# A decoder layer on one core: the cumulative product's idle operand, and the norm of a stick-breaking unit

## The chip, the cores and the metric

The kernel runs on one core of one Trainium2 chip. The core has TensorE (PE: matmuls; PEld is its weight load), VectorE (DVE), ScalarE (ACT), GpSimd (POOL) and SyncE (SP), whose queue issues the DMAs. The metric is the time of one execution in microseconds on the device. Before the change it is 3093.26 us, the median of three runs (3088.63 to 3095.98).

## What is computed

One decoder layer over 2048 positions of width 1024, in f32. A norm and one projection give queries, keys and values. Four heads do differential attention, with a softmax. Eight heads of width 64 do stick-breaking attention. The outputs are joined, projected, normed and added; a gated MLP with a short convolution follows, and has the larger half of the matmuls. The part that matters here is this, cut from the reference:

```python
z = jnp.einsum('bhqd,bhkd->bhqk', q_blk, k).astype(jnp.float32) * scale
log_beta = jax.nn.log_sigmoid(z)
log_1mb = jnp.where(strict, jax.nn.log_sigmoid(-z), 0.0)
between = lax.cumsum(log_1mb, axis=3, reverse=True) - log_1mb
a = jnp.where(strict, jnp.exp(log_beta + between), 0.0)
return jnp.einsum('bhqk,bhkd->bhqd', a.astype(v.dtype), v)
...
sb_o = _rmsnorm(_stick_breaking_attention(sq, sk, sv), sb_norm[l])
```

Each query row needs, for every key, the product of sigmoid(-z) over the later keys: the kernel works with sigmoids and a running product in place of logarithms and sums. Each head's 64 outputs are then normed and multiplied by the 64 gains sb_norm.

## The kernel before

**Stages.** Projection passes go first (L605, L602). From then on, attention and the remaining projections are merged step by step, so that projection matmuls fill TensorE's gaps: differential attention for four pairs of heads, then stick-breaking for four pairs. The output projection (L1101) is merged into the end of stick-breaking, and the MLP (L1226, L1311) comes last. A unit is a pair of heads g with 256 query rows s; stick-breaking has 32 units.

**Order of work.** The code doesn't issue instructions as it runs. Each step is an operation with an engine (or two to choose from), a cost, its dependencies and its buffers, and a planner (class `Plan`) lays them out when the kernel is built: an engine takes the oldest ready operation whose buffers fit. So the order on each engine's queue is fixed at build, and at run time each engine follows its queue and waits on semaphores. Buffers are counted: z has three PSUM banks, t (transposes) two, o and g a few more. A PSUM buffer is marked `bank`, and the planner does not start an operation on it while another engine's is under way. `copy` may go to ACT or DVE.

**Stick-breaking, per chunk.** A chunk is up to 512 keys of one head for 128 rows; there are 320 (224 with 512 keys, 32 each with 384, 256 and 128). In `front`: L702 computes z into PSUM, two matmuls, since the query is split in a high and a low part (L705 adds the mask on the diagonal); L969 writes sigmoid(-z) to the tile gm in SBUF and L971 sigmoid(z) to the tile be, both on ACT; L977 is the running product over gm, backward, on DVE, in place, starting from the chunk before (`carry`); L982 multiplies be by it on POOL. gm and be are parts of two rings of SBUF, `a` and `w`. Two units later the rows are transposed (L720), evacuated as high part (L466 or L467) and low part (L734), and multiplied with the values into o (L1000).

The product, with its operand gm read twice and the second one not used (`bypass`):

```python
gr = gm.t[:, 0:w + 1][:, ::-1]
nc.vector.tensor_tensor_scan(gr, gr, gr, 1.0 if cb is None else cb[0].t[:, 0:1],
                             ALU.mult, ALU.bypass)
```

**Stick-breaking, the end of a unit.** `fin_sb` (L793) evacuates o, transposes it in four pieces (L799), and gets for each query row and each of four pieces 64 values twice, from the high and the low part of the value product. A copy takes the second half and L804 (DVE) adds the first; L806 squares (POOL), L807 sums (DVE), L382 scales and adds epsilon (DVE), L384 takes the power -1/2 (POOL), and L816, four times, multiplies a piece by its row's factor and by the gains, which lie in `sbn` across all partitions. `mix_out` (L758) transposes the result (L763), copies it to SBUF and stores it. `mix_out` is also used by differential attention (`fin_diff`, L768).

Of the kernel before, what the change touches and what calls it, by code (L numbers as in the profile page):

```python
# [24 lines left out]
P = 128  # L25
# [241 lines left out]
def layer_kernel(  # L267
# [167 lines left out]
    def setup_rest():  # L435
# [11 lines left out]
        mem["sbn"] = load(lambda: sbn, sb_norm[0:1, :].to_broadcast([P, 64]), 32768)  # L447
# [310 lines left out]
    def mix_out(g, s, mx, deps):  # L758
# [6 lines left out]
        o = copy(lambda: mo.t, lambda: ps.t[:, 0:256], 256, (o,), (ps, mo))  # L765
# [27 lines left out]
    def fin_sb(g, s, po, last):  # L793
        ot, pq, os_, ss, sq, mx = buf("ot"), buf("t"), buf("os"), small(), buf("sq"), buf("mix")
# [6 lines left out]
        p4 = lambda: pq.t.rearrange("p (c l d) -> p c l d", c=4, l=2)  # L801
        o4 = lambda: os_.t.rearrange("p (c d) -> p c d", c=4)
# [3 lines left out]
        o = op("POOL", c_pool(256), lambda: nc.gpsimd.tensor_tensor(sq.t, os_.t, os_.t, ALU.mult), (o,), (os_, sq))  # L806
        o = op("DVE", 335, lambda: nc.vector.reduce_sum(ss.t[:, 0:4], sq.t.rearrange("p (c d) -> p c d", c=4),  # L807
                                                        axis=AX.X), (o,), (sq, ss))
        r, o = rs_ops(lambda: ss.t[:, 0:4], 64, 4, (o,), (ss,))

        def fin():
            m4 = mx.t.rearrange("p (j m d) -> p j m d", j=2, m=2)
            for m in range(2):
                for jj in range(2):
                    c = m * 2 + jj
# [612 lines left out]
```

## Time and profile before

| what | value |
|---|---|
| median of 3 runs | 3093.26 us |
| the profiled execution | 3094.23 us |
| its span in the profile | 3092.5 us |
| PE busy | 2984.5 us (97%) |
| DVE busy | 2252.0 us (73%) |
| ACT busy | 1442.9 us (47%) |
| POOL busy | 951.6 us (31%) |
| mean granted TensorE clock | 0.992 of full |

The profile is of one execution. An engine is busy while an instruction's record lasts, so a record that contains a wait inside the engine counts as busy, and matmul records overlap, their ends being modelled. The shares are averages over stages with different limits; the tables by stretch of time are what to read; there, behind the engines, stand the granted clock as a share, the share of the DMA engines and GB/s. In a row of a group, "xcount | busy, mean ns | idle before" is followed by what ended the idle time.

### The profile page before, as it was taken

The page shows a single profiled execution, that of the slowest core. Times are in us where ns is not written, and L with a number is a line of the kernel's source. Part 1 is how long each engine was busy: PE and PEld are TensorE (multiplying, and loading weights), DVE is VectorE, ACT ScalarE, POOL GpSimd, SP SyncE. Part 2 cuts the span into 40 slices and gives each one's busy share as a digit, 9 for nine tenths or more (in the row PEclk, how much of TensorE's full clock was granted, in tenths as well). Part 3 has the DMA queues.
Part 4 walks back from the last instruction along what each step waited for, and adds up shares of the span by engine and source line. Part 5 has one row for each costly group of instructions (what it writes and reads, how often), then busy time and mean ns, then how long its engine had stood idle before and what let it go on. Part 6 is the DMA issues. An engine that isn't in the chain of part 4 may idle for free. (4 is left out here: it accounts for less than half of the span.)

```text
span 3092.5 us, 48117 instructions
## 1 busy us (share of the span) xinstructions
PE 2984.5 (97%) x17352; PEld 2610.4 (84%) x17352; DVE 2252.0 (73%) x4327; ACT 1442.9 (47%) x2913; POOL 951.6 (31%) x1047
## 2 busy tenths in 40 slices
PE   7999999999999999889999999999999999999998
PEld 7899999999888888868877888888888888888887
DVE  4658878897999999998754864387744776277742
ACT  4434545555777767666643433233322433233321
POOL 1001002002766777675411211033301332023310
PEclk9999999999999999999999999999999999999999
DMA  8776656655634366533363333443344333343332
GB/s 264 246 209 186 185 151 201 171 156 159 188 122 130 95 194 185 151 100 112 110 214 126 102 100 116 121 134 96 96 129 143 96 99 106 119 141 101 96 123 82
DMA packets 392146, 437.11 MB, mean 141 GB/s; under 512 B 20096, under 2 KB 328164, under 8 KB 381668
## 3 DMA queue, kind: packets, MB, share of 16 engines
q1 hardware_dynamic: 391908, 434.05, 46.7%
q8 instruction: 136, 2.23, 0.3%
q14 instruction: 102, 0.84, 0.1%
HBM read 333.30 MB, written 100.67 MB: 140 GB/s over the span
## 5 line engine op out<-in xcount | busy, mean ns | idle before, releaser
L1226 PE MATMUL pu<-fh,fhi 128*128 128x512 f32 x2816 | 869.0, 390 | 0.2 <-ACT fu L1234 0.2
L1226 PEld LDWEIGHTS pu<-fh,fhi 128*128 128x128 f32 x2816 | 529.4, 188 | 110.5 <-ACT fu L1234 0.6
L461 DVE TENSOR_TENSOR flo<-fraw,fhi 128x1024 fp32r<-128x1024 f32 x186 | 233.0, 1254 | 488.6 <-ACT fhi L458 488.5
L1226 PE MATMUL pu<-fh,flo 128*128 128x512 f32 x1408 | 549.2, 390 | 0.0
L982 POOL TENSOR_TENSOR ring_w<-ring_w,ring_a 128x512 f32<-128x512 f32 (+2 forms) x320 | 387.9, 1224 | 220.3 <-DVE ring_a L977 121.1
L605 PE MATMUL g<-hT,big 128*128 128x256 f32 x3072 | 447.8, 288 | 7.3 <-DVE st L638 4.3
L458 ACT CAST fhi<-fraw 128x1024 fp32r<-128x1024 f32 x253 | 265.5, 1051 | 397.4 <-PE py L1311 218.6
L1311 PE MATMUL py<-fhi,gt 128*128 128x512 f32 x1408 | 435.9, 390 | 0.0
L605 PEld LDWEIGHTS g<-hT,big 128*128 128x128 f32 x3072 | 405.4, 192 | 19.8 <-DVE st L638 4.4
L977 DVE TENSOR_TENSOR_SCAN ring_a<-ring_a 128x513 f32<-128x513 f32 (+2 forms) x320 | 412.8, 1316 | 6.1 <-ACT ring_a L969 6.1
L702 PE MATMUL z<-k,q 128*128 128x512 f32 (+3 forms) x1280 | 362.5, 376 | 10.4 <-ACT ring_a L969 7.0
L466 ACT CAST thi<-t 128x512 fp32r<-128x512 f32 (+2 forms) x472 | 221.6, 492 | 210.1 <-PE t L720 179.3
L1311 PEld LDWEIGHTS py<-fhi,gt 128*128 128x128 f32 x1408 | 264.5, 188 | 60.0
L1226 PEld LDWEIGHTS pu<-fh,flo 128*128 128x128 f32 x1408 | 264.7, 188 | 54.9
L734 DVE TENSOR_TENSOR tlo<-t,thi 128x512 fp32r<-128x512 f32 (+2 forms) x528 | 281.6, 556 | 34.6 <-ACT thi L466 28.4
L459 POOL TENSOR_TENSOR flo<-fraw,fhi 128x1024 fp32r<-128x1024 f32 x78 | 195.8, 2510 | 338.9 <-DVE fhi L457 171.2
L1311 PE MATMUL py<-flo,gt 128*128 128x512 f32 x704 | 277.8, 395 | 0.0
L720 PE MATMUL t<-ident,ring_w 128*128 128x128 f32 x1632 | 253.2, 276 | 22.4 <-DVE tlo L734 18.5
L1250 POOL TENSOR_TENSOR gt<-fy,gt 128x512 fp32r<-128x512 f32 x88 | 118.4, 1347 | 493.9 <-ACT gt L1249 483.0
L1239 DVE SCALAR_TENSOR_TENSOR fy<-fu,cw,fy 128x512 f32<-128x512 f32 x176 | 239.6, 1361 | 6.2
L384 POOL TENSOR_TENSOR sm<-sm,neghalf 128x2 f32<-128x2 f32 (+1 forms) x72 | 76.8, 1067 | 536.5 <-DVE sm L382 534.7
L602 PE MATMUL g<-big,hT 128*128 128x256 f32 x1536 | 227.4, 288 | 6.3 <-DVE st L624 1.5
(158 smaller groups left out, 4697.4 us busy)
## 6 DMA issues: line engine op xcount, KB each, us to landing
fraw<-in_w_up_dram SPq DMA_DIRECT2D x176, 512.0 KB, 3.8
hT<-hd SPq DMA_DIRECT2D x64, 1024.0 KB, 7.0
fraw<-in_w_down_dram SPq DMA_DIRECT2D x88, 512.0 KB, 3.8
q<-qd SPq DMA_DIRECT2D x128, 256.0 KB, 4.3
hd<-hT SPq DMA_DIRECT2D x16, 1024.0 KB, 5.4
qd<-st SPq DMA_DIRECT2D x128, 128.0 KB, 2.6
kd<-st SPq DMA_DIRECT2D x128, 128.0 KB, 2.6
vd<-st SPq DMA_DIRECT2D x64, 256.0 KB, 5.2
```

Of the source, the lines that this page charges most:

```text
L458: "ACT", c_act(n) + 42, lambda: nc.scalar.copy(hi(), raw()))
L461: "DVE", c_dvs(n), lambda: nc.vector.tensor_tensor(lo(), raw(), f32(hi()), ALU.subtract))
L602: nc.tensor.matmul(ps.t[:, cs], hk[:, b, c * P:(c + 1) * P], wv[:, a, k, :], start=first, stop=last)
L605: nc.tensor.matmul(ps.t[:, cs], wv[:, a, k, c * P:(c + 1) * P], hk[:, b, :], start=first, stop=last)
L702: nc.tensor.matmul(ps.t[:, 0:w], q.t[:, m, l, jj * P:(jj + 1) * P], kt.t[:, m, 0:w], start=(l == 0), stop=(l == 1 and not masked))
L720: nc.tensor.transpose(ps.t[:, cc * P:(cc + 1) * P], rows[jj].t[:, (k + kk) * P:(k + kk + 1) * P], ident)
L734: ol = op("DVE", c_dvp(n), lambda sl=sl: nc.vector.tensor_tensor(lo.t[:, sl], ps.t[:, sl], f32(hi.t[:, sl]), ALU.subtract), (oh,), (ps, hi ...
L977: nc.vector.tensor_tensor_scan(gr, gr, gr, 1.0 if cb is None else cb[0].t[:, 0:1], ALU.mult, ALU.bypass)
L982: rdeps.append(op("POOL", c_pool(w), lambda be=be, gm=gm, w=w: nc.gpsimd.tensor_tensor(be.t, be.t, gm.t[:, 1:w + 1], ALU.mult), (o1, o2), ...
L1226: nc.tensor.matmul(ps.t, w3(w)[:, k, :], h.t[:, a, k, :], start=(k == 0 and i == 0), stop=(k == KD - 1 and i == 2))
L1239: nc.vector.scalar_tensor_tensor(y.t, u.t[:, 1:TT + 1], cw[:, 1, f:f + 1], y.t, ALU.mult, ALU.add)
L1311: nc.tensor.matmul(ps.t, gt.t[:, a, j * P:(j + 1) * P], wt.t[:, ms], start=(m == 0 and i == 0), stop=(m == NFT - 1 and i == 2))
```

## The change

The product's second operand becomes the first column of the z tile in PSUM, repeated; the product thus reads that tile and is one of its users. In a unit's end, the four transposes become four multiplications with `fold`, an identity of 64 stacked on itself, which adds the two halves; a plain copy evacuates the sum. The scale of the mean and the epsilon move to one POOL operation, with 64 and the factor 8 taken into `sbn`, which now holds the gains down the partitions, twice. One DVE operation multiplies all four pieces by their row factors. The gains are applied in `mix_out` by the evacuation after the transpose, where they lie down the partitions: on ACT, or on DVE.

```diff
-    sbn = const.tile([P, 64], F32, name="sbn")
+    sbn = const.tile([P, 1], F32, name="sbn")
+    fold = const.tile([P, 64], F32, name="fold")
+    nc.vector.tensor_tensor(fold, ident[:, 0:64], ident[:, 64:P], ALU.add)
...
-        mem["sbn"] = load(lambda: sbn, sb_norm[0:1, :].to_broadcast([P, 64]), 32768)
+        ls = [load(lambda m=m: sbn[m * 64:(m + 1) * 64], sb_norm.rearrange("o p -> p o"), 256) for m in range(2)]
+        mem["sbn"] = op("DVE", 75, lambda: nc.vector.tensor_scalar(sbn, sbn, 8.0, None, ALU.mult), ls)
...
+        if scale is None:
+            o = copy(lambda: mo.t, lambda: ps.t[:, 0:256], 256, (o,), (ps, mo))
+        else:
+            o = op("ACT", c_act(256) + 95, lambda: nc.scalar.activation(
+                mo.t, ps.t[:, 0:256], AF.Identity, scale=sbn[:, 0:1]), (o, scale), (ps, mo)).alt(
+                "DVE", c_dvp(256), lambda: nc.vector.tensor_scalar(mo.t, ps.t[:, 0:256], sbn[:, 0:1], None, ALU.mult))
...
-                nc.tensor.transpose(pq.t[:, c * P:(c + 1) * P], ot.t[:, c * P:(c + 1) * P], ident)
+                nc.tensor.matmul(pq.t[:, c * 64:(c + 1) * 64], ot.t[:, c * P:(c + 1) * P], fold, start=True, stop=True)
...
-        o = copy(o4, lambda: p4()[:, :, 1, :], 256, (o,), (pq, os_))
-        o = op("DVE", c_dvp(256), lambda: nc.vector.tensor_tensor(o4(), p4()[:, :, 0, :], o4(), ALU.add), (o,),
-               (pq, os_))
+        o = copy(lambda: os_.t, lambda: pq.t[:, 0:256], 256, (o,), (pq, os_))
...
-        r, o = rs_ops(lambda: ss.t[:, 0:4], 64, 4, (o,), (ss,))
+        def pw():
+            nc.gpsimd.tensor_scalar(t.t[:, 0:4], ss.t[:, 0:4], 64 * EPS, None, ALU.add)
+            nc.gpsimd.tensor_tensor(r.t[:, 0:4], t.t[:, 0:4], neghalf[:, 0:4], ALU.pow)
+        o1 = op("POOL", 1200, pw, (o1,), (ss, t, r))
...
-                    nc.vector.scalar_tensor_tensor(m4[:, jj, m, :], o4()[:, c, :], r.t[:, c:c + 1], sbn,
-                                                   ALU.mult, ALU.mult)
-        o = op("DVE", 4 * 196, fin, (o, mem["sbn"]), (r, os_, mx))
+            nc.vector.tensor_tensor(
+                mx.t.rearrange("p (j m d) -> p j m d", j=2, m=2),
+                os_.t.rearrange("p (m j d) -> p j m d", m=2, j=2),
+                r4.unsqueeze(3).to_broadcast([P, 2, 2, 64]), ALU.mult)
+        o = op("DVE", 396, fin, (o1,), (r, os_, mx))
+        mix_out(g, s, mx, (o,), mem["sbn"])
...
-                    nc.vector.tensor_tensor_scan(gr, gr, gr, 1.0 if cb is None else cb[0].t[:, 0:1],
-                                                 ALU.mult, ALU.bypass)
-                o1 = op("DVE", c_scan(w), scan, [o0, o1] + ([cb[1]] if cb else []), [gm] + ([cb[0]] if cb else []),
-                        what="scan")
+                    nc.vector.tensor_tensor_scan(gr, gr, ps.t[:, 0:1].to_broadcast([P, w + 1]),
+                                                 1.0 if cb is None else cb[0].t[:, 0:1], ALU.mult, ALU.bypass)
+                o1 = op("DVE", c_scan(w), scan, [o0, o1] + ([cb[1]] if cb else []),
+                        [gm, ps] + ([cb[0]] if cb else []), what="scan")
```

## Rows read from the trace of the kernel before

**Rows 1.** Stretches: us; busy us (instructions) of PE, PEld, DVE, ACT, POOL; then the clock.

```profile
250.00:450.00 200.00, 199.84 (x1547) 192.44 (x1546) 169.16 (x574) 97.30 (x215) 11.25 (x11) 1.00 0.62 170
738.00:800.00 62.00, 61.57 (x500) 59.80 (x500) 48.21 (x84) 36.56 (x96) 29.57 (x46) 1.00 0.66 189
800.00:1350.00 550.00, 503.07 (x3721) 460.64 (x3720) 537.61 (x779) 401.37 (x914) 397.12 (x561) 0.99 0.51 151
1350.00:1531.00 181.00, 168.01 (x945) 141.46 (x944) 154.98 (x219) 112.46 (x275) 104.58 (x137) 0.97 0.30 98
...
1700.00:3092.50 1392.50, 1383.44 (x6082) 1142.44 (x6080) 856.79 (x1223) 463.75 (x655) 320.99 (x181) 1.00 0.37 111
```

**Rows 2.** DVE's groups by line, stretch 738 to 1531 (first two: L977).

```profile
L977 DVE TENSOR_TENSOR_SCAN ring_a<-ring_a 128x513 f32<-128x513 f32 (+2 forms) x320 | 412.8, 1316 | 6.1 <-ACT ring_a L969 6.1
...
L977 DVE TENSOR_TENSOR_SCAN ring_a<-ring_a 128x513 f32<-128x513 f32 x224 | 327.7, 1481 | 4.5 <-ACT ring_a L969 4.5
...
L816 DVE SCALAR_TENSOR_TENSOR mix<-os,sm,sbn 128x64 f32<-128x64 f32 x124 | 54.4, 497 | 3.2 <-POOL ring_a L967 2.3 <-POOL sm L384 0.8
...
L804 DVE TENSOR_TENSOR os<-t,os 128x256 f32<-128x256 f32 x31 | 12.5, 403 | 1.5 <-ACT os L466 1.3
L382 DVE TENSOR_SCALAR sm<-sm 128x4 f32<-128x4 f32 (+1 forms) x32 | 12.2, 380 | 0.5 <-ACT sq L780 0.4
```

**Rows 3.** Timeline of DVE and POOL: start us, us, instruction.

```profile
1006.85 1.28 DVE L977 TENSOR_TENSOR_SCAN ring_a<-ring_a 128x513 f32<-128x513 f32 x1
1008.04 1.69 DVE L816 SCALAR_TENSOR_TENSOR mix<-os,sm,sbn 128x64 f32<-128x64 f32 x4
...
1016.40 1.47 DVE L977 TENSOR_TENSOR_SCAN ring_a<-ring_a 128x513 f32<-128x513 f32 x1
...
1018.38 1.46 DVE L977 TENSOR_TENSOR_SCAN ring_a<-ring_a 128x513 f32<-128x513 f32 x1
...
1002.30 1.09 POOL L982 TENSOR_TENSOR ring_w<-ring_w,ring_a 128x512 f32<-128x512 f32 x1 [1.11 <-PE z L702]
...
1016.79 1.98 POOL L982 TENSOR_TENSOR ring_w<-ring_w,ring_a 128x512 f32<-128x512 f32 x1
```

**Rows 4.** TensorE's transposes of attention rows, 800 to 1350, then 250 to 450.

```profile
L720 PE MATMUL t<-ident,ring_w 128*128 128x128 f32 x849 | 132.5, 276 | 14.6 <-DVE tlo L734 12.7 <-DVE sm L382 0.5 <-DVE os L804 0.4
...
L720 PE MATMUL t<-ident,ring_w 128*128 128x128 f32 x178 | 27.1, 273 | 0.0
```

**Rows 5.** First sigmoids (L969, two rows), products (L977, two rows) since 738, counted.

```profile
738.00:950.00 212.00, 50.42 (x96) 1.00 0.56 165
...
738.00:1200.00 462.00, 110.52 (x210) 1.00 0.52 154
...
738.00:950.00 212.00, 113.94 (x90) 1.00 0.56 165
...
738.00:1200.00 462.00, 258.83 (x203) 1.00 0.52 154
```

**Rows 6.** Waits, whole span: who for whom, us in total, times, longest.

```profile
POOL ring_w L982 <- DVE ring_a L977: 121.1, 88, 3.5
...
ACT r L1117 <- DVE r L1115: 13.3, 8, 3.8
```

**Rows 7.** Groups by line and shape, whole span (L422: its source view).

```profile
L971 ACT ACTIVATE ring_w<-z 128x512 f32<-128x512 f32 x224 | 134.0, 613 | 9.0 <-PE z L702 7.7 <-PE z L705 0.6
...
L574 ACT ACTIVATE hT<-t,g_pre 128x256 fp32r<-128x256 f32 x64 | 25.9, 473 | 29.3 <-PE t L567 19.3 <-PE g L602 9.9
...
L734 DVE TENSOR_TENSOR tlo<-t,thi 128x512 fp32r<-128x512 f32 x336 | 223.2, 676 | 29.9 <-ACT thi L466 26.0 <-PE o L911 1.5 <-PE o L1000 1.2
...
L1248 DVE TENSOR_TENSOR fy<-fy,fy 128x512 f32<-128x512 f32 x88 | 65.2, 742 | 2.8 <-DVE fu L1232 0.4
...
L384 POOL TENSOR_TENSOR ws<-ws,neghalf 128x1 f32<-128x1 f32 x32 | 21.0, 656 | 66.6 <-DVE ws L382 61.9 <-DVE fu L1232 4.8
...
L422 PE MATMUL t<-ring_w,sm x2: 481/482/482, 87.0 to 87.3; 32*4 32x384 f32 x2
```

More of the change, by code (lines that the diff above doesn't have):

```diff
@@ L756, in layer_kernel, with mix_out @@
     mixs = {}
-    def mix_out(g, s, mx, deps):
+    def mix_out(g, s, mx, deps, scale=None):
         ps, mo = buf("t"), buf("mo")
@@ L793, in fin_sb @@
     def fin_sb(g, s, po, last):
-        ot, pq, os_, ss, sq, mx = buf("ot"), buf("t"), buf("os"), small(), buf("sq"), buf("mix")
+        ot, pq, os_, ss, sq, mx, r = buf("ot"), buf("t"), buf("os"), small(), buf("sq"), buf("mix"), small()
         o = copy(lambda: ot.t, lambda: po.t, 512, (last,), (po, ot))
@@ L804, in fin_sb @@
-        o = op("DVE", c_dvp(256), lambda: nc.vector.tensor_tensor(o4(), p4()[:, :, 0, :], o4(), ALU.add), (o,),
-               (pq, os_))
-        o = op("POOL", c_pool(256), lambda: nc.gpsimd.tensor_tensor(sq.t, os_.t, os_.t, ALU.mult), (o,), (os_, sq))
-        o = op("DVE", 335, lambda: nc.vector.reduce_sum(ss.t[:, 0:4], sq.t.rearrange("p (c d) -> p c d", c=4),
-                                                        axis=AX.X), (o,), (sq, ss))
-        r, o = rs_ops(lambda: ss.t[:, 0:4], 64, 4, (o,), (ss,))
@@ L811, in fin @@
-        def fin():
[L812 to L815, printed above, removed]
-                    nc.vector.scalar_tensor_tensor(m4[:, jj, m, :], o4()[:, c, :], r.t[:, c:c + 1], sbn,
-                                                   ALU.mult, ALU.mult)
-        o = op("DVE", 4 * 196, fin, (o, mem["sbn"]), (r, os_, mx))
-        mix_out(g, s, mx, (o,))
+        o = copy(lambda: os_.t, lambda: pq.t[:, 0:256], 256, (o,), (pq, os_))
@@ new lines, in fin_sb @@
+        o1 = op("POOL", c_pool(256), lambda: nc.gpsimd.tensor_tensor(sq.t, os_.t, os_.t, ALU.mult), (o,), (os_, sq))
+        o1 = op("DVE", 335, lambda: nc.vector.reduce_sum(ss.t[:, 0:4], sq.t.rearrange("p (c d) -> p c d", c=4),
+                                                         axis=AX.X), (o1,), (sq, ss))
+        t = small()
+        def pw():
+            nc.gpsimd.tensor_scalar(t.t[:, 0:4], ss.t[:, 0:4], 64 * EPS, None, ALU.add)
+            nc.gpsimd.tensor_tensor(r.t[:, 0:4], t.t[:, 0:4], neghalf[:, 0:4], ALU.pow)
@@ L821, in layer_kernel @@
+        o1 = op("POOL", 1200, pw, (o1,), (ss, t, r))
+        def fin():
+            r4 = r.t[:, 0:4].rearrange("p (m j) -> p j m", m=2)
+            nc.vector.tensor_tensor(
[4 more added lines that the diff above has]
+        mix_out(g, s, mx, (o,), mem["sbn"])
     LEAD = {"z": 0.0, "ev": 0.0}
@@ L973, in front, with scan @@
                 cb = None if diag else carry[m, jj]
-                def scan(gm=gm, w=w, cb=cb):
+                def scan(gm=gm, w=w, cb=cb, ps=ps):
                     gr = gm.t[:, 0:w + 1][:, ::-1]
-                    nc.vector.tensor_tensor_scan(gr, gr, gr, 1.0 if cb is None else cb[0].t[:, 0:1],
-                                                 ALU.mult, ALU.bypass)
-                o1 = op("DVE", c_scan(w), scan, [o0, o1] + ([cb[1]] if cb else []), [gm] + ([cb[0]] if cb else []),
-                        what="scan")
+                    nc.vector.tensor_tensor_scan(gr, gr, ps.t[:, 0:1].to_broadcast([P, w + 1]),
+                                                 1.0 if cb is None else cb[0].t[:, 0:1], ALU.mult, ALU.bypass)
+                o1 = op("DVE", c_scan(w), scan, [o0, o1] + ([cb[1]] if cb else []),
+                        [gm, ps] + ([cb[0]] if cb else []), what="scan")
                 carry[m, jj] = (gm, o1)
```

3 lines of the change are left out of this document (removed).

## The prediction

> **What bounds the kernel now.** I read the table of stages first. From 1700 us to the end, in the MLP, TensorE is busy 1383.44 of 1392.50 us, so nothing there can be gained by VectorE work [rows 1]. Stick-breaking runs from 738 to 1531 us. TensorE is busy 61.57 of 62 us in the first stretch, but 503.07 of 550 and 168.01 of 181 us in the next two: 0.4 + 46.9 + 13.0 = 60.3 us idle. VectorE is busy 537.61 of the 550 us (98%); ScalarE has 401 and POOL 397. The stretch 250 to 450, in differential attention, is what to hold beside it: VectorE at 85% (169.16 of 200) and TensorE never idle [rows 1]. So between 800 and 1350 VectorE sets the pace.
>
> Next, what VectorE does there. The cumulative products (L977) are 412.8 us, and the norm of a unit (L804, L382, L816) 12.5 + 12.2 + 54.4 us [rows 2]. A product over 513 elements costs 327.7/224 = 1.46 us on average, though alone it takes 1.19 us to the next start (1006.85 to 1008.04). The timeline shows why: while POOL multiplies, each product reads 1.46 or 1.47 us and the POOL instruction 1.98 us in place of 1.09 [rows 3]. The two engines' records overlap, and the lengths add up as if they took turns. Both instructions read two SBUF operands. The evacuation of the same size with one PSUM operand (L734) has a mean of 0.676 us, below the 0.742 us of a two-SBUF one (L1248) [rows 7].
>
> **The change, part by part.**
>
> *The product's unused operand.* The multiplication and the bypass stay, but the second stream comes from a PSUM column. If turn-taking with POOL goes, 224 products save 1.46 - 1.19 = 0.27 us: 61 us. The 96 shorter ones take (412.8 - 327.7)/96 = 0.89 us; they have 257 elements on average, half of 513, so an estimate from 1.19 us is about 0.64 with a fixed part, and they save 0.25 each: 24 us. Together 85 us of VectorE. The price of the PSUM read is not in the trace. From below: nothing, and no further gain beyond the 0.066 us that separates L734 from L1248, 320 times, 21 us. From above: the read costs as much as a whole L734 beside the product, 1.19 + 0.68 = 1.87 us, then 224 products lose 0.41 each and the short ones (0.64 + 0.34 against 0.89) 0.09 each: 92 + 9 = 101 us worse. I take nothing, since a product spends 1.19/513 = 2.3 ns per element and L734, which reads PSUM, 1.3 ns: the stream from PSUM keeps up. POOL gains too: its 512-element multiplications go from 1.98 towards 1.09 us wherever they stood behind a product; POOL isn't the bound, so I count nothing.
>
> [...]
>
> *The norm.* Per unit, VectorE loses the addition of halves (0.403), the scale-and-add (12.2/32 = 0.38) and four operations (54.4/31 = 1.75) [rows 2], 2.54 us, and gets one operation over 256 elements with two SBUF inputs. That is 0.40 us as L804, or 0.7 if it waits for POOL; I take 0.5. So 2.0 us for each of 31 units in the stage: 63 us. POOL gets a four-element add: between nothing and the 0.656 us of its smallest power operation [rows 7], at most 32 x 0.66 = 21 us, in an engine with 793 - 471 = 322 us free (29.57 + 397.12 + 104.58 busy) [rows 1]. ScalarE's last evacuation now scales: 0.473 us for that shape [rows 7], at most 32 x 0.47 = 15 us if all came new; they are there already as copies, so it is a fraction, and ScalarE is busy 550 of 793 [rows 1]. TensorE's four transposes become four multiplications by a folded identity, 64 columns wide. The only plain f32 product of the trace, 384 columns, is two matmuls of 0.48 us [rows 7]; a sixth of it is about 0.16, against a transpose of 0.276 us as the trace books it [rows 4]. Two passes in place of one make it even, give or take 0.1 us, 128 times: 13 us either way at most, taken as nothing. The norm's chain also gets shorter, but the units overlap, so I count nothing for latency.
>
> *Setup.* One 32 KB load becomes two of 256 bytes on SP, one issue more, long before the stage begins; one small VectorE operation doubles as its scale, and one builds the fold while VectorE waits for its first data. All under 1 us, hidden by the first loads; uncovered they would cost that 1 us.
>
> *Buffers and waits.* The product now reads the z tile. A bank of z, of which there are three, is free for the next z only after the product, no longer after the second sigmoid. Also, the two readers of one bank are kept apart: the product stands behind the second sigmoid (0.613 us) [rows 7]. Behind a standing product in VectorE's queue are the low-part subtractions that TensorE's value products wait for; behind a z standing on TensorE is everything. In the trace, ScalarE runs ahead: 96 sigmoids against 90 products by 950 us, 210 against 203 by 1200 [rows 5]. At most three chunks can be ahead after the change. That lead is VectorE's backlog; with 148 us of its work gone I expect it to shrink, and no cost.
>
> **The sum.** VectorE in the stage: 48.21 + 537.61 + 154.98 = 740.8, less 85 and 63, is 593 us of 793. That is no bound: it is 81% of a stage of 728 us, where 250 to 450 ran a full TensorE beside 85%. So TensorE is next. If 800 to 1350 ran at the pace of 250 to 450 (200/1547 = 0.129 us per matmul), its 3721 would take 481 us: 69 us less. The mix is not the same (849 transposes in 3721 against 178 in 1547 [rows 4]), so this is an estimate. The idle time shown is 46.9. I take the middle, 58. In 1350 to 1531, where the projections that fill gaps have ended, 13.0 us are idle and VectorE has 155 of 181: I take half, 7. Nothing before 800 or after 1531. Sum 65 us. The profiled execution took 3094.2 us (span 3092.5 and 1.7 around it), 1.0 above the median of 3093.3: 3094.2 - 65 = 3029 us.
>
> **The rivals.**
>
> 1. *Three z banks become the bound* (slower). The loop is z, two sigmoids, product, then z again. With nothing queued it is two matmuls at the stage's pace, 0.26, two sigmoids, 1.23, and the product, 1.19: 2.7 us and the handovers, so some 0.9 us per chunk, against 793/320 = 2.48 now. It decides once the queues of ScalarE and VectorE and the handovers add 4.7 us, a loop of 7.43 us. At 8 us it gives 320 x 8/3 = 853 us, 60 more: 3154 us. For it: today's lead of six or seven chunks [rows 5] is over 14 us of flight. Against it: that is backlog, and differential attention turns the same three banks with TensorE full.
>
>    Reads of one bank by two engines follow each other already: ScalarE stood 13.3 us for VectorE's read of one tile in L1115 to L1117, where neither needs the other's result [rows 6]. [...]
>
> 2. *The product gets dearer.* At the upper price VectorE has 740.8 + 101 - 63 = 779 us, still the bound: no gain, 3080 to 3100 us. For it: no product from PSUM is in the trace. Against it: 1.3 against 2.3 ns per element.
>
> 3. *A chain holds the stage.* POOL stood 121.1 us for products, in 88 waits [rows 6]; product, multiplication, transpose and evacuation are one chain. If the order was made for other lengths and the TensorE stalls stay half, the gain is some 30 us: 3064 us.
>
> 4. *The contention stays*, that is, the operand change doesn't do what it says. The norm alone leaves 740.8 - 63 = 678 us; the stage shortens by some 30 us at most, 3064 us again.
>
> **How the numbers follow.** The forecast has 0.70, the third and fourth rivals together 0.14, the banks 0.10, the dear product 0.06. The time is that of the first, 3029. Its own range goes from all of 69 + 13 us plus the 21 us by which the PSUM read could be cheaper (3094 - 103 = 2991) to a gain of 30. Including half-gains and a dear product that still leaves something, 2990 to 3080 holds 8 in 10; the banks and a full loss stand outside it. About 0.2%, 6 us, is what a measurement of this kernel can tell from no change. Faster: 0.70 + 0.14 and a third of the dear product, 0.86. Within 0.2%: 0.04. Slower: 0.10.
>
> **What would show it.** In the new profile, right: products of 513 elements at 1.2 to 1.3 us beside a POOL multiplication of 1.1; VectorE near 590 us between the first and last product; that stretch 720 to 740 us long; TensorE idle under 20 us in its middle 550. Wrong: TensorE waiting at z (L702) for the product; products of 1.5 us or more; VectorE waiting at the product for the second sigmoid, for tens of us. The forecast falls if the stretch stays above 765 us.

## The result, and the profile after

| | before | after |
|---|---|---|
| median of the runs, us | 3092.52 (3088.63 to 3095.98) | 3034.05 (3031.72 to 3037.15) |
| profiled execution / its span, us | 3094.2 / 3092.5 | 3037.15 / 3035.4 |
| first product begins, us from the start | 738.0 | 740.1 |
| first to last product (the stage), us | 782.1 | 715.6 |
| from the last product to the end, us | 1572.4 | 1579.7 |

The changed kernel takes 0.9815 of the time, with a 95% interval of 0.9802 to 0.9827: 58.5 us less. The span is 57.1 us shorter: the stage gains 66.5 us, its start is 2.0 us later, and the rest, in which nothing was meant to change, takes 7.3 us more (66.5 - 2.0 - 7.3, but for rounding).

The stage first. This is the table of stretches of the changed kernel; the columns are those of [rows 1]. The first row is the whole stage.

```profile
740.10:1455.70 715.60, 705.68 (x5223) 659.56 (x5222) 628.65 (x946) 532.48 (x1242) 423.04 (x765) 1.00 0.51 155
...
800.00:1350.00 550.00, 540.08 (x4118) 509.38 (x4117) 496.46 (x734) 427.74 (x983) 342.99 (x633) 1.00 0.53 160
1350.00:1456.00 106.00, 106.00 (x618) 91.55 (x617) 90.95 (x140) 70.13 (x172) 55.13 (x87) 1.00 0.32 109
1456.00:1531.00 75.00, 69.92 (x341) 57.78 (x341) 42.10 (x75) 34.84 (x94) 15.29 (x22) 0.98 0.63 203
```

The whole stage in the same view of the kernel before:

```profile
738.00:1520.10 782.10, 722.47 (x5096) 652.80 (x5095) 733.95 (x1069) 545.01 (x1268) 528.99 (x739) 0.99 0.47 142
```

Between 800 and 1350 us TensorE is now busy 540.08 of 550 us with 4118 instructions, where it had 503.07 with 3721. VectorE has 496.46 (before 537.61). Over the stage VectorE falls from 733.95 to 628.65 us, POOL from 528.99 to 423.04. POOL's fall is as large as VectorE's, although the change gives POOL work rather than takes it away.

The groups by line show why. L987 is the product (L977 before), L823 the norm's one operation, L470 an evacuation that ScalarE or VectorE may write. The row with "(+2 forms)" is all 320 products. Columns as in [rows 2].

```profile
L987 DVE TENSOR_TENSOR_SCAN ring_a<-ring_a,z 128x513 f32<-128x513 f32 x224 | 276.6, 1259 | 8.9 <-ACT ring_w L980 5.2 <-issue 2.0 <-POOL ring_w L992 1.0
...
L470 DVE CAST thi<-t 128x512 fp32r<-128x512 f32 x59 | 40.4, 688 | 22.9 <-PE t L723 22.5
...
L823 DVE TENSOR_TENSOR mix<-os,sm 128x256 f32<-128x256 f32 x32 | 21.0, 655 | 2.4 <-POOL sm L818 2.4
...
L987 DVE TENSOR_TENSOR_SCAN ring_a<-ring_a,z 128x513 f32<-128x513 f32 (+2 forms) x320 | 338.9, 1084 | 17.4 <-ACT ring_w L980 11.9 <-issue 2.5 <-POOL ring_w L992 2.1
...
L992 POOL TENSOR_TENSOR ring_w<-ring_w,ring_a 128x512 f32<-128x512 f32 x224 | 249.1, 1113 | 147.4 <-DVE ring_a L987 112.2 <-PE t L723 11.7 <-PE o L1010 7.4
...
L818 POOL TENSOR_TENSOR sm<-sm,neghalf 128x4 f32<-128x4 f32 x32 | 33.1, 1036 | 2.7
...
L811 POOL TENSOR_TENSOR sq<-os 128x256 f32<-128x256 f32 x32 | 20.1, 629 | 35.1 <-ACT os L469 23.7 <-DVE os L470 9.3 <-DVE tlo L737 1.9
```

The same evacuation and POOL's three groups in that view of the kernel before, the multiplication under L982, the power under L384, the squares under L806:

```profile
L467 DVE CAST thi<-t 128x512 fp32r<-128x512 f32 x44 | 30.0, 685 | 10.0 <-PE t L720 9.9
...
L982 POOL TENSOR_TENSOR ring_w<-ring_w,ring_a 128x512 f32<-128x512 f32 x224 | 302.6, 1360 | 164.7 <-DVE ring_a L977 92.1 <-ACT ring_w L971 27.2 <-PE t L720 14.1
...
L384 POOL TENSOR_TENSOR sm<-sm,neghalf 128x4 f32<-128x4 f32 x32 | 42.2, 1318 | 6.7 <-DVE sm L382 5.2
...
L806 POOL TENSOR_TENSOR sq<-os 128x256 f32<-128x256 f32 x32 | 35.0, 1095 | 1.7 <-DVE os L804 1.5
```

A product of 513 elements has gone from 1.481 us [rows 2] to 1.259, POOL's multiplication from 1.360 to 1.113, the power operation from 1.318 to 1.036, the squares from 1.095 to 0.629. All that shared the time with the product got shorter, also where the change left it alone. The timeline (start in us, length in us, instruction) shows the two engines side by side, where [rows 3] had 1.47 against 1.98:

```profile
1002.72 1.27 DVE L987 TENSOR_TENSOR_SCAN ring_a<-ring_a,z 128x513 f32<-128x513 f32 x1
...
1004.23 1.27 DVE L987 TENSOR_TENSOR_SCAN ring_a<-ring_a,z 128x513 f32<-128x513 f32 x1
...
1004.13 1.12 POOL L992 TENSOR_TENSOR ring_w<-ring_w,ring_a 128x512 f32<-128x512 f32 x1 [0.83 <-PE t L723]
...
1005.64 1.09 POOL L992 TENSOR_TENSOR ring_w<-ring_w,ring_a 128x512 f32<-128x512 f32 x1 [0.35 <-PE z L705]
```

The view of the waits has one that answers to [rows 6], and those that the change could bring, for the second sigmoid and for a bank of z (L705):

```profile
POOL ring_w L992 <- DVE ring_a L987: 166.4, 127, 9.7
...
DVE ring_a L987 <- ACT ring_w L980: 11.9, 21, 1.5
...
PEld z L705 <- DVE ring_a L987: 7.5, 11, 1.8
...
PE z L705 <- DVE ring_a L987: 4.5, 7, 1.6
```

TensorE's weight loads wait for the product 7.5 us in all, its matmuls 4.5 us of that same time; the product stands 11.9 us for the second sigmoid, now that the two readers of a bank are kept apart. The lead of the sigmoids over the products, six and seven in [rows 5], is 2 and 3 (100 against 98 by 950 us, 227 against 224 by 1200).

What TensorE's matmuls waited for is in the same view, taken from 738 to 1531 us. Before:

```profile
PE t L720 <- DVE tlo L734: 18.1, 18, 2.7
...
PE t L763 <- DVE tlo L734: 13.9, 15, 2.0
```

And after, where these lines are L723, L766 and L737:

```profile
PE t L766 <- DVE tlo L737: 1.6, 1, 1.6
...
PE t L723 <- DVE tlo L737: 1.2, 3, 0.7
```

Before, 32.0 of the 59.6 us for which TensorE stands idle in the stage (782.10 - 722.47) end with a low-part subtraction, an instruction in VectorE's queue, where the products stand too. So VectorE's queue is what TensorE waited for; after, TensorE is idle for 9.9 us in all.

The 7.3 us that were given back lie in the MLP. These are the two groups of matmuls of its second half, by line and shape, of the kernel after:

```profile
L1321 PE MATMUL py<-fhi,gt 128*128 128x512 f32 x1408 | 440.6, 393 | 0.0
...
L1321 PE MATMUL py<-flo,gt 128*128 128x512 f32 x704 | 280.9, 399 | 0.0
```

And of the kernel before:

```profile
L1311 PE MATMUL py<-fhi,gt 128*128 128x512 f32 x1408 | 435.9, 390 | 0.0
...
L1311 PE MATMUL py<-flo,gt 128*128 128x512 f32 x704 | 277.8, 395 | 0.0
```

The instructions are the same, the clock is 1.00 in both, and TensorE has nothing to wait for; still the 2112 matmuls take 440.6 + 280.9 - 435.9 - 277.8 = 7.8 us more. From one start to the next it is 233.3 ns on average instead of 228.9, 4.4 ns for each of 2107 pairs of neighbours, 9.4 us. No edit touches that code. The last experiment takes this up.

### The profile page after: what moved, and what is told of

Read it like the earlier page. It is cut to its first block, busy times and chain, and to the rows that moved or that the text cites. A ratio compares the mean times of both kernels' runs of the same rounds, so it can differ in the third digit from the quotient of the medians.

```text
span 3035.4 us, 48333 instructions
## 1 busy us (share of the span) xinstructions
PE 2979.0 (98%) x17480; PEld 2617.2 (86%) x17480; DVE 2144.1 (71%) x4199; ACT 1430.5 (47%) x2887; POOL 847.0 (28%) x1075
## 4 chain that ended last, share of the span: by engine, by line
PE 49%; DVE 1%; issue 0%; ACT 0%; POOL 0%; POOLq 0%; ACTq 0%
PE pu L1236 31%; PE py L1321 16%; PE g L1111 2%; DVE fy L1258 0%; PE t L1149 0%; DVE halo L1245 0%; DVE fy L1248 0%; DVE fy L1249 0%; DVE fy L1250 0%; POOL gt L1260 0%; DVE o L1304 0%; ACT r L1155 0%; ACT r L1127 0%; DVE fu L1242 0%; DVE o L1292 0%
## 5 line engine op out<-in xcount | busy, mean ns | idle before, releaser
L461 ACT CAST fhi<-fraw 128x1024 fp32r<-128x1024 f32 x253 | 265.9, 1052 | 406.6 <-PE py L1321 226.7
L1321 PE MATMUL py<-fhi,gt 128*128 128x512 f32 x1408 | 440.6, 393 | 0.0
L992 POOL TENSOR_TENSOR ring_w<-ring_w,ring_a 128x512 f32<-128x512 f32 (+2 forms) x320 | 311.1, 976 | 205.8 <-DVE ring_a L987 166.4
L705 PE MATMUL z<-k,q 128*128 128x512 f32 (+3 forms) x1280 | 360.9, 373 | 7.6 <-DVE ring_a L987 4.5
L987 DVE TENSOR_TENSOR_SCAN ring_a<-ring_a,z 128x513 f32<-128x513 f32 (+2 forms) x320 | 338.9, 1084 | 17.4 <-ACT ring_w L980 11.9
L737 DVE TENSOR_TENSOR tlo<-t,thi 128x512 fp32r<-128x512 f32 (+2 forms) x528 | 282.6, 559 | 49.1 <-ACT thi L469 41.5
L469 ACT CAST thi<-t 128x512 fp32r<-128x512 f32 (+2 forms) x453 | 211.1, 493 | 172.8 <-PE t L723 143.4
L1321 PE MATMUL py<-flo,gt 128*128 128x512 f32 x704 | 280.9, 399 | 0.0
L723 PE MATMUL t<-ident,ring_w 128*128 128x128 f32 x1632 | 250.0, 273 | 3.2 <-DVE tlo L737 1.6
L605 PEld LDWEIGHTS g<-big,hT 128*128 128x128 f32 x1536 | 205.5, 192 | 10.8 <-POOL big L462 1.7
```

The costliest lines, as they stand in the source:

```text
L461: "ACT", c_act(n) + 42, lambda: nc.scalar.copy(hi(), raw()))
L605: nc.tensor.matmul(ps.t[:, cs], hk[:, b, c * P:(c + 1) * P], wv[:, a, k, :], start=first, stop=last)
L705: nc.tensor.matmul(ps.t[:, 0:w], q.t[:, m, l, jj * P:(jj + 1) * P], kt.t[:, m, 0:w], start=(l == 0), stop=(l == 1 and not masked))
L723: nc.tensor.transpose(ps.t[:, cc * P:(cc + 1) * P], rows[jj].t[:, (k + kk) * P:(k + kk + 1) * P], ident)
L737: ol = op("DVE", c_dvp(n), lambda sl=sl: nc.vector.tensor_tensor(lo.t[:, sl], ps.t[:, sl], f32(hi.t[:, sl]), ALU.subtract), (oh,), (ps, hi ...
L987: nc.vector.tensor_tensor_scan(gr, gr, ps.t[:, 0:1].to_broadcast([P, w + 1]), 1.0 if cb is None else cb[0].t[:, 0:1], ALU.mult, ALU.bypass)
```

## The experiments

Twelve kernels ran. "Shift" says whether the SBUF tiles behind `sbn` lie 32 bytes higher than in the kernel before (the last run tests it). Stage and rest are as in the table above; the ratio is to the kernel before, on the same chip.

| run | the product's second operand | norm | else | shift | stage, us | rest, us | median, us | ratio (95%) |
|---|---|---|---|---|---|---|---|---|
| before | SBUF | old | | no | 782.1 | 1572.4 | 3092.5 | 1 |
| after | PSUM | new | | yes | 715.6 | 1579.7 | 3034.1 | 0.9815 (0.9802 to 0.9827) |
| e1 | PSUM | old | | no | 723.6 | 1569.8 | 3032.3 | 0.9811 (0.9796 to 0.9825) |
| e2 | SBUF | new | | yes | 768.7 | 1583.6 | 3092.7 | 1.0005 (0.9995 to 1.0014) |
| e3 | SBUF | new | order of after | yes | 768.7 | 1581.2 | 3087.7 | 0.9989 (0.9980 to 0.9999) |
| e4 | PSUM | new | half products | yes | 709.6 | 1582.3 | 3029.7 | 0.9808 (0.9793 to 0.9823) |
| e5 | SBUF | old | half products | no | 707.6 | 1571.3 | 3018.3 | 0.9773 (0.9756 to 0.9789) |
| e6 | PSUM | new | two z banks | yes | 729.5 | 1581.5 | 3053.1 | 0.9887 (0.9873 to 0.9902) |
| e7 | SBUF | old | two z banks | no | 779.4 | 1572.2 | 3095.4 | 1.0018 (1.0009 to 1.0027) |
| e8 | SBUF | old | half low part | no | 757.6 | 1570.6 | 3064.5 | 0.9922 (0.9908 to 0.9937) |
| e9 | PSUM | new | products ahead | yes | 722.8 | 1582.4 | 3041.9 | 0.9852 (0.9837 to 0.9866) |
| e10 | SBUF | new | half products | yes | 712.0 | 1585.8 | 3034.0 | 0.9825 (0.9811 to 0.9840) |
| e11 | SBUF | old | half multiplications | no | 718.0 | 1571.0 | 3027.2 | 0.9803 (0.9787 to 0.9819) |
| e12 | PSUM | new | addresses of before | no | 716.1 | 1570.0 | 3025.7 | 0.9790 (0.9776 to 0.9803) |

### Which of the two parts? (e1, e2, e3)

e1 is the kernel before with the product's new operand alone:

```diff
-                    nc.vector.tensor_tensor_scan(gr, gr, gr, 1.0 if cb is None else cb[0].t[:, 0:1],
-                                                 ALU.mult, ALU.bypass)
-                o1 = op("DVE", c_scan(w), scan, [o0, o1] + ([cb[1]] if cb else []), [gm] + ([cb[0]] if cb else []),
-                        what="scan")
+                    nc.vector.tensor_tensor_scan(gr, gr, ps.t[:, 0:1].to_broadcast([P, w + 1]),
+                                                 1.0 if cb is None else cb[0].t[:, 0:1], ALU.mult, ALU.bypass)
+                o1 = op("DVE", c_scan(w), scan, [o0, o1] + ([cb[1]] if cb else []),
+                        [gm, ps] + ([cb[0]] if cb else []), what="scan")
```

> Only the product's second operand is changed; the norm stays as before. Theory A (VectorE set the pace of stick-breaking and TensorE does after it): products at 1.26 us, VectorE about 667 us of work in the stage, already under what TensorE needs, so most of the 58 us: a gain of 40 to 58, 3035 to 3052 us. Theory B (both parts give time in proportion to the VectorE work they save, 74 and 60 us): a gain of about 32, 3060 us.

e2 is the changed kernel with the product as it was, in operand and in users (the reverse of that diff).

> Only the norm is changed; the product reads its SBUF operand twice as before. Theory A: products stay at 1.4 to 1.5 us, VectorE about 680 us of work, close to what TensorE needs; a gain of 30 to 50, 3042 to 3062 us, and with the run of the operand alone more than the whole 58. Theory B: about 26, 3066 us.

e3 keeps all of the changed kernel, the planned order of every queue too, and puts back only the operand:

```diff
-                    nc.vector.tensor_tensor_scan(gr, gr, ps.t[:, 0:1].to_broadcast([P, w + 1]),
+                    nc.vector.tensor_tensor_scan(gr, gr, gr,
```

> The changed kernel, every queue in its order, only the product's second operand is the SBUF one again; the z bank stays counted as held for it by the planner. Turn-taking with POOL as the cause: products go back to 1.4 us or more wherever POOL multiplies, VectorE to 690 to 700 us of work, the time to 3045 to 3070 us. The planner's new order as the cause: products may get longer, the time stays at 3034 us within 6.

The groups of the product and of POOL's multiplication, and the whole stage in the table of stretches, of e1:

```profile
L978 DVE TENSOR_TENSOR_SCAN ring_a<-ring_a,z 128x513 f32<-128x513 f32 x224 | 277.1, 1259 | 7.1 <-ACT ring_w L971 5.6 <-POOL sq L806 0.5 <-issue 0.4
...
L983 POOL TENSOR_TENSOR ring_w<-ring_w,ring_a 128x512 f32<-128x512 f32 x224 | 249.6, 1115 | 189.1 <-DVE ring_a L978 114.5 <-PE t L720 27.3 <-PE o L1001 12.6
...
737.00:1460.70 723.70, 704.56 (x5099) 647.93 (x5098) 663.57 (x1088) 535.66 (x1250) 418.62 (x739) 1.00 0.50 153
```

The same of e2, with the norm's operation (L823):

```profile
L986 DVE TENSOR_TENSOR_SCAN ring_a<-ring_a 128x513 f32<-128x513 f32 x224 | 326.6, 1481 | 5.1 <-ACT ring_a L978 4.9
...
L823 DVE TENSOR_TENSOR mix<-os,sm 128x256 f32<-128x256 f32 x32 | 32.4, 1013 | 9.6 <-POOL sm L818 8.6 <-POOL ring_a L976 0.9
...
L991 POOL TENSOR_TENSOR ring_w<-ring_w,ring_a 128x512 f32<-128x512 f32 x224 | 305.4, 1374 | 128.3 <-DVE ring_a L986 77.0 <-PE t L723 12.7 <-ACT ring_w L980 11.8
...
733.90:1502.50 768.60, 725.64 (x5220) 666.88 (x5218) 701.93 (x919) 549.81 (x1271) 533.89 (x762) 0.99 0.47 144
```

The operand alone gives all that the change gives, 0.9811 against 0.9815, and a little more than e1's first theory allowed (3032.3 against 3035 to 3052). The norm alone missed both of e2's theories: it gives nothing that can be told from no change, 1.0005 (0.9995 to 1.0014), though its records show that it does what it should: the four scaled copies are one operation. That operation, 0.655 us in the changed kernel, takes 1.013 us here, and the products stay at 1.481. e3, with 768.7 us of stage as in e2, says that the other order of the queues is not what made the difference; the operand is. It lost more than either of its theories said (3087.7 against 3045 to 3070, or 3034): without the operand next to nothing of the gain is left.

The operand's mechanism is the one of the prediction. e1 shows it in the means: with one input in PSUM both are shorter, the product 1.481 to 1.259 us and POOL's multiplication 1.360 to 1.115.

The trace of the kernel before shows the turns one by one, when its records are sorted by what the other engine has under way at their start (POOL's small writes, L967, left out). Of the 224 products of 513 elements, 45 have nothing of POOL beside them: 1.274 us, the median. 58 are under way when POOL starts: 1.256. The other 121 start while POOL is at work. Of these, 12 start beside a power operation (L384), which holds none of them up: 1.271; the other 109 have a median of 1.709 and go up to 2.665. POOL's 224 multiplications of 512 elements take 1.091 us with no product beside them, 1.092 where the product starts later, and 1.900 where one is already under way. So whoever comes second waits, and the first is not slowed. The wait is what the first has left: the 92 of the 109 for which POOL had more than 0.25 us to go lasted that rest plus 1.08 to 1.09 us. In the changed kernel the classes without POOL, before POOL and after POOL have 1.272, 1.255 and 1.271 us, and the multiplications 1.095, 1.096 and 1.094: neither waits for the other.

### Is VectorE the bound, then or now? (e4, e5)

The product over half of each chunk's keys, in the kernel before (e5) and likewise in the changed one (e4, where the repeated column is cut to the same length):

```diff
-                    gr = gm.t[:, 0:w + 1][:, ::-1]
+                    gr = gm.t[:, 0:w + 1][:, ::-1][:, 0:w // 2 + 1]
```

> The changed kernel, with the product over the last half of each chunk's keys only; the other half is left out. It takes about 130 us of VectorE work out of the stage and nothing else; the planned order is the same. Theory A (TensorE is the bound now): 3024 to 3034 us. If VectorE were still the bound: 60 us or more less, under 2975 us.

> The kernel before, with the product over the last half of each chunk's keys only; the other half is left out. Theory A (VectorE was the bound): some 150 to 200 us of VectorE work less, as the turns with POOL get shorter too, and the time falls to TensorE's limit, 3020 to 3045 us. A chain of waits as the bound: 3060 to 3080 us.

The whole stage in the table of stretches, of e4:

```profile
732.70:1442.30 709.60, 702.09 (x5216) 658.89 (x5215) 507.45 (x946) 530.86 (x1241) 417.72 (x765) 1.00 0.51 156
```

And of e5:

```profile
736.20:1443.90 707.70, 693.98 (x5088) 646.29 (x5087) 574.83 (x1069) 536.80 (x1266) 447.83 (x739) 1.00 0.52 156
```

In the changed kernel 121 us less of VectorE (628.65 to 507.45) shorten the stage by 6 us and the run by 4: VectorE is no longer the bound, and the 702.09 us for which TensorE is busy are. In the kernel before, 159 us less of VectorE (733.95 to 574.83) shorten the stage by 74.5 us, to 708 us, of which TensorE is busy for 694; the run, 3018.3, is just under the 3020 to 3045 expected. e5 therefore can't say by itself whether it was VectorE's time or the turns with POOL that fell away, since a half product shortens both: the product goes from 1.481 to 0.887 us, POOL's multiplication from 1.360 to 1.177.

### VectorE's own time, or the turns? (e8, e11)

Two more kernels separate them, both from the kernel before. e8 takes work from VectorE that POOL doesn't lengthen, the low-part subtraction, which reads PSUM (its mean in the stage is 0.551 us before and 0.556 after; in the kernel before, those of 512 elements have a median of 0.680 us with nothing of POOL beside them and of 0.674 where POOL is already at work):

```diff
+    for tl in T["tlo"].tiles:
+        nc.vector.memset(f32(tl), 0.0)
...
-            ol = op("DVE", c_dvp(n), lambda sl=sl: nc.vector.tensor_tensor(
-                lo.t[:, sl], ps.t[:, sl], f32(hi.t[:, sl]), ALU.subtract), (oh,), (ps, hi, lo), what="lo")
+            sh = slice(sl.start, sl.start + n // 2)
+            ol = op("DVE", c_dvp(n), lambda sh=sh: nc.vector.tensor_tensor(
+                lo.t[:, sh], ps.t[:, sh], f32(hi.t[:, sh]), ALU.subtract), (oh,), (ps, hi, lo), what="lo")
```

> The kernel before, with the subtraction that makes the low part done over half of its columns; the other half of the low part is left out (zeros). It takes some 70 us from VectorE's own busy time in the stage, all of it in instructions that read PSUM. Theory A (VectorE's own time set the pace before): 3030 to 3050 us. Theory P (the pace was set by the turns that VectorE's instructions with two SBUF operands and POOL's instructions take at each other; an instruction of VectorE that reads PSUM takes no turn): no gain to speak of, 3075 to 3095 us, and POOL's multiplications and the products stay at 1.37 and 1.46 us or so.

e11 takes nothing from VectorE and half of POOL's multiplication:

```diff
-                    be.t, be.t, gm.t[:, 1:w + 1], ALU.mult), (o1, o2), (be, gm), what="mul"))
+                    be.t[:, 0:w // 2], be.t[:, 0:w // 2], gm.t[:, 1:w // 2 + 1], ALU.mult), (o1, o2), (be, gm), what="mul"))
```

> The kernel before, with POOL's multiplication over half of each chunk's keys (the rest is left unmultiplied). It takes some 120 us or more of POOL's time out; VectorE's instructions are the same. Theory P: POOL's turns were in the way of VectorE's, so the stage shortens until TensorE bounds it, 3025 to 3050 us, with products of 1.35 to 1.45 us. If only VectorE's own work counted (products of 1.27 us when nothing is beside them, the rest unchanged): 3065 to 3080 us. If POOL had nothing to do with it: 3090 us.

The kernel before has this for the low parts of the stage, all shapes together, in the groups by line:

```profile
L734 DVE TENSOR_TENSOR tlo<-t,thi 128x512 fp32r<-128x512 f32 (+2 forms) x356 | 187.1, 551 | 12.0 <-ACT thi L466 8.3 <-PE o L911 1.9 <-PE o L1000 1.2
```

e8 has this for them (L737), then for the products, POOL's multiplications and the stage:

```profile
L737 DVE TENSOR_TENSOR tlo<-t,thi 128x256 fp32r<-128x256 f32 (+2 forms) x356 | 115.0, 347 | 17.4 <-ACT thi L468 14.3 <-PE o L914 2.0 <-PE o L1003 0.5
...
L980 DVE TENSOR_TENSOR_SCAN ring_a<-ring_a 128x513 f32<-128x513 f32 x224 | 343.9, 1553 | 3.8 <-ACT ring_a L972 3.7
...
L985 POOL TENSOR_TENSOR ring_w<-ring_w,ring_a 128x512 f32<-128x512 f32 x224 | 323.3, 1453 | 135.0 <-DVE ring_a L980 65.6 <-ACT ring_w L974 32.3 <-PE t L722 10.2
...
732.10:1489.60 757.50, 710.57 (x5096) 650.56 (x5094) 687.01 (x1069) 544.21 (x1268) 550.11 (x739) 0.99 0.48 146
```

e11's products, scaled copies of the norm (L816), halved multiplications and stage:

```profile
L977 DVE TENSOR_TENSOR_SCAN ring_a<-ring_a 128x513 f32<-128x513 f32 x224 | 297.2, 1345 | 4.0 <-ACT ring_a L969 3.9
...
L816 DVE SCALAR_TENSOR_TENSOR mix<-os,sm,sbn 128x64 f32<-128x64 f32 x128 | 40.1, 373 | 2.1 <-POOL sm L384 1.1 <-POOL ring_a L967 1.0
...
L982 POOL TENSOR_TENSOR ring_w<-ring_w,ring_a 128x256 f32<-128x256 f32 x224 | 192.4, 868 | 199.4 <-DVE ring_a L977 103.0 <-ACT ring_w L971 33.6 <-PE t L720 17.9
...
736.50:1454.50 718.00, 696.00 (x5089) 643.91 (x5089) 663.99 (x1069) 539.67 (x1266) 391.40 (x739) 1.00 0.51 154
```

e8 came out between the theories, at 3064.5 us, in neither range. The stage's low parts lose 72 us (187.1 to 115.0), and the stage 24.5. A part of the rest came back as longer turns: VectorE's busy time fell by 47 us only (733.95 to 687.01), for the products went from 1.481 to 1.553 us (16 us over 224), the multiplications from 1.360 to 1.453. So VectorE's own time counted, at a third of its length.

e11 gave nearly the whole gain of the change, 0.9803, without touching an instruction of VectorE: 718.0 us of stage, and 3027.2 in all, in theory P's range. Its products fell to 1.345 us and the four scaled copies from 0.490 to 0.373, because POOL held them up less. VectorE's 663.99 us in the stage are those of e1 (663.57). That POOL, busy for 528.99 of 782.1 us before, could have been shortened for nothing is refuted. e11 also shortens the chain from product to multiplication to transpose, but that chain was hardly waited for: in the kernel before, TensorE's weight loads stood 2.0 us for multiplications in the whole stage.

What the two sizes say together is in part open. The turns by themselves did not fill the stage before: the records of POOL (its small writes left out) and of VectorE's instructions with two SBUF inputs, laid over each other, cover 698 of its 782 us. What set the pace was VectorE's queue, which has to pass both its own work and its standing, and which read busy for 733.95 us, 94%. Of that, e11 takes 70 us, and the stage gives 64; e8 takes 47 and it gives 24.5; e2 takes 32 (701.93) and it gives 13.4. Why so much less of it comes through in e8 and e2 was not tested. What the tables show is that in these two VectorE stands idle for some 20 us more (70.5 and 66.7 us, where it was 48.2 before), and in e11 for 6 more (54.0).

### The z banks (e6, e7, e10, e9)

With two banks of z in place of three, in the changed kernel (e6) and in the one before (e7):

```diff
-    for name, n in (("z", 3), ("o", 1), ("g", 2)):
+    for name, n in (("z", 2), ("o", 1), ("g", 2)):
```

> The changed kernel with two z banks in place of three, for both kinds of attention. If banks are far from binding: within 15 us of 3034. If the product's hold of the bank is near the bound (two banks leave a loop of 4.5 us per chunk pair): 60 us or more, over 3094 us.

> The kernel before with two z banks in place of three, where a bank is free after the second sigmoid. It is the control of the two-bank run: what two banks cost without the product's hold. Banks far from binding: within 15 us of 3093. The difference of the two losses is the price of the hold.

TensorE's waits at z for the product, in e6's view of the waits:

```profile
PEld z L705 <- DVE ring_a L987: 13.1, 19, 2.7
...
PE z L705 <- DVE ring_a L987: 7.7, 14, 2.5
```

A bank fewer costs the changed kernel 19 us by the medians (3053.1 against 3034.1) and the kernel before 3 to 8 (0.09 to 0.27% of 3092). So e6 lies between its two expectations, and e7 within its 15 us. The difference, some 13 us, is the price of the longer hold with two banks; the weight loads' waits for the product show 5.6 us of it (13.1 against 7.5), and where the rest lies was not looked into. With three banks, e10 asks for the price: the norm's part alone, half products, so that nothing holds the bank.

> The norm's part alone (the product's second operand is its SBUF tile again, so a z bank is free after the second sigmoid), with the product over half of each chunk's keys; the other half is left out. Beside the changed kernel with half products (3030 us) it differs in the operand and so in how long a z bank is held. If the hold costs something: 3012 to 3020 us, like the kernel before with half products (3018). If it costs nothing, and the norm's order of work made the difference between those two: 3027 to 3033 us.

It takes 3034.0 us where e4, with the hold, takes 3029.7. The hold costs nothing that shows, though e10's products also take turns with POOL again (0.875 us, against 0.732 in e4), and a few us could hide behind that. That e5 was 11 us faster than e4 is its rest, 1571.3 against 1582.3 us, and not the banks. The order of e9, which gives the banks back sooner, is no gain either:

```diff
-                    gm.t[:, 0:w], ps.t[:, 0:w], AF.Sigmoid, scale=-1.0), (o,), (gm, ps), LEAD["ev"], what="sig")
+                    gm.t[:, 0:w], ps.t[:, 0:w], AF.Sigmoid, scale=-1.0), (o,), (gm, ps), 4e3, what="sig")
...
-                        [gm, ps] + ([cb[0]] if cb else []), what="scan")
+                        [gm, ps] + ([cb[0]] if cb else []), 4e3, what="scan")
```

> The changed kernel, with the two sigmoids and the product put ahead in the planner's order (a lead of 4000 ns each), so that a z bank is given back sooner. If the hold of the z banks is what is left to gain: 3020 to 3030 us, with the waits of z for the product under 5 us. If TensorE's own work bounds the stage: 3032 to 3036 us.

The stage in e9's table of stretches:

```profile
734.50:1457.40 722.90, 711.50 (x5215) 661.77 (x5215) 626.30 (x942) 534.75 (x1243) 418.27 (x763) 0.99 0.51 153
```

The waits of z for the product hardly changed (5.2 us at the weight loads and 5.9 at the matmuls), the stage got 7 us longer, and the run 8 by the medians, 11 by the ratios, which neither theory said. Of the matmuls' 5.9 us, 4.5 are a single stall, at 1303 us, which the weight loads' row puts down to ScalarE's work on another tile (L461, 5.0 us, once). Why the other order is worse was not looked into further.

### The MLP's 9 us (e12)

All seven traces with the new norm so far had the longer groups and a rest of 1579.7 us or more; all six with the old one had the shorter ones and a rest under 1573. The norm's operations are long over by then. What stays is the layout: `sbn` shrank from 256 bytes per partition to 4, and `fold` takes 256, so each tile laid out behind them starts higher, by 32 bytes: the traces hold no addresses, but the programs built from the two kernels do, and in them the first of the `fhi` tiles goes from 65056 to 65088 (65056 again in e12). Of the operands of these matmuls that moves `fhi` and `flo`, while `gt` is laid out from the other end and stays (139232 in all three). e12 puts the scale column into a spare column of another tile:

```diff
-    sbn = const.tile([P, 1], F32, name="sbn")
...
-    nc.gpsimd.memset(neghalf, -0.5)
+    nc.gpsimd.memset(neghalf[:, 0:4], -0.5)
+    sbn = neghalf[:, 4:5]
```

> The changed kernel, with the norm's scale column kept in a spare column of the tile of exponents, so that the tiles that are laid out behind it lie where they lay in the kernel before, 32 bytes lower than in the changed kernel; the work is the same. In the traces so far every kernel with the new norm has 440.6 and 280.9 us in the two groups of matmuls of the MLP's second half, and every kernel with the old one 435.8 and 277.5 or so, and its span goes on for 1580 to 1586 us after the last product instead of 1570 to 1573. If the 32 bytes are the cause: groups of 435.9 and 277.8, a rest of 1570 to 1573 us after the last product, and 3023 to 3028 us in all. If the norm's operations or the order of work make it: groups of 440.6 and 280.9, and 3032 to 3037 us.

The two groups and the stage of e12:

```profile
L1321 PE MATMUL py<-fhi,gt 128*128 128x512 f32 x1408 | 435.8, 390 | 0.0
...
L1321 PE MATMUL py<-flo,gt 128*128 128x512 f32 x704 | 277.4, 394 | 0.0
...
738.50:1454.60 716.10, 706.31 (x5223) 659.83 (x5222) 628.86 (x946) 532.50 (x1242) 422.44 (x765) 1.00 0.51 155
```

The groups are back at 435.8 and 277.4 us, the rest at 1570.0, and the stage is what it was: the places of the tiles are the cause, as the first of e12's theories had it. With 3025.7 us, 0.9790 (0.9776 to 0.9803), this is the fastest complete kernel of the study: 66 us under the kernel before, 8 under the changed one. The same 32 bytes had hidden what the norm is worth: against e1, at the addresses of before in both, it is 7.5 us of stage (723.6 to 716.1) and 6.6 us of median. The norm alone, e2, had gained 13.4 us in the stage and lost them behind it.

## Why the prediction was right, and where it was not

The time, 3029 us, was 5 us under the 3034 measured, and a gain of 65 us in the stage stands against 66.5 there. The sum was better than its terms, and that is in part luck. Once VectorE's queue is short enough, TensorE's own work sets the stage's length, so it hardly matters how much more VectorE saves (in e4 121 us less of it shorten the stage by 6); and the forecast's 58 + 7 us, a middle between TensorE's idle time and a pace taken from another stage, came close to what TensorE gave: 49.7 us less idle time (59.6 to 9.9) and 16.8 us less busy time (722.47 to 705.68).

**Right.** The mechanism: a product with both streams in SBUF takes turns with POOL's work, and one with a stream in PSUM does not (those that start while POOL is at work, its power operation left out, have a median of 1.709 us before; in the changed kernel all that start so have 1.271). The products at 1.2 to 1.3 us beside a multiplication of 1.1 (1.259 and 1.113). The PSUM read at no price, as the rows had it: 1.272 us against 1.274 for the undisturbed products before. The short ones too fell, from 85.1 to 62.3 us in all (412.8 - 327.7 against 338.9 - 276.6), 22.8 saved of 24 forecast. TensorE as the next bound, idle 9.9 us in the middle 550, under the 20 named. The new waits at z and at the second sigmoid small, 7.5 and 11.9 us, so the first rival did not happen with three banks; e6 shows that it has a place, with two.

**"So between 800 and 1350 VectorE sets the pace": right of the queue, half of the cause.** TensorE did wait for VectorE's queue. The prediction also saw that the products stood for POOL, and priced that. But the step "POOL isn't the bound, so I count nothing" put the length of POOL's work at nothing, though it is what VectorE stands for: a product that comes second lasts as long as POOL's rest and 1.08 us. e11 shortens POOL alone and gets 60.7 us (0.9803); e8 takes 72 us of VectorE's own work and gets 24. POOL's free time was also added up wrongly: 793 less 29.57 + 397.12 + 104.58 is 262 us, not 322.

**The norm's term, 63 us of VectorE, and the fourth rival's "norm alone", 30 us.** VectorE did lose most of it: 12.5 + 12.2 + 54.4 [rows 2] against 20.5 us for the 31 of L823 in the stage, 58.6. But alone, in e2, it took only 32 us off VectorE's busy time (733.95 to 701.93), with its one operation standing for POOL (1.013 us where 0.5 was forecast and the changed kernel has 0.655, and 0.415, the median of six, with nothing of POOL beside it), and only 13.4 us off the stage; once the products were out of the way it gave 7.5 to 8. The forecast needed both terms only because it priced them in the same coin, VectorE's time; the first alone was enough to make TensorE the bound.

**VectorE near 590 us between the products: 628.65.** The products saved 73.9 us (412.8 to 338.9), not 85: 1.19 was the distance to the next start, 1.26 is a product's record. The norm saved 58.6, not 63. And more evacuations went to VectorE: in the stage 32 where there were 14, 18.2 us where there were 7.1 (of the largest shape, over the whole span, 30.0 to 40.4). Some 16 us of the difference lie in smaller groups and in records that overlap less. The stretch from first to last product, 715.6 us, is a little under the 720 to 740 named.

**"Nothing before 800 or after 1531": wrong by 7 us.** A ninth of the stage's gain was given back in a stage that the change doesn't touch. No step of the prediction asked what tiles of another size do to the places of the others.

## What to carry to other kernels

Where two engines' records get longer beside each other, sort them by which engine started first: if only the second is longer (here 1.709 us, against 1.256 for a product that came first), they take turns, and part of what reads busy is standing. Then don't price the engine that reads busy alone. Make a test kernel that shortens the other engine's part, and one that takes work from the busy engine beside the turns: here 60.7 us against 24. When an edit changes the size of a tile, compare the matmul groups of stages that it doesn't touch (here 440.6 us against 435.9), and try the old places, before its worth is judged.

## What was not expected of the hardware

- A shift of the tiles `fhi` and `flo` by 32 bytes changes the pace of matmuls of 512 float32 columns with a clock of 1.00 and no waits: 228.9 ns from start to start in each of the seven traces with the places of before (e12's among them), 233.3 in each of the seven with the others, 2%. The matmuls of the MLP's first half, which read `fh` and take `fhi` and `flo` as weights, did not change (227.1 and 227.2 ns), though `fh`, laid out just ahead of them, moved as well. Whether the place itself counts or its distance to `gt`, which did not move, was not tried.
- A product that reads its second stream from PSUM, repeated from one column, costs no more than one from SBUF that nothing holds up: 1.272 us, the median of the 52 that have nothing of POOL beside them in the changed kernel, against 1.274 of 45 before.
- An operand that an operation doesn't use (the bypass) still made it take turns with POOL: e3 and the changed kernel differ in nothing else, and their products of 513 elements take 1.493 and 1.259 us.
